# A bias table from a split bias, reciprocals spread by split diagonals, and the conformer's variance beside the last values' products

## The chip, the cores and the metric

The kernel runs on one core of a Trainium2 chip. The metric is device time in microseconds (us), the median of several executions. Within a core TensorE (PE) multiplies matrices, VectorE (DVE), ScalarE (ACT) and GpSimd (POOL) work on elements, and SyncE (SP) issues most of the loads. Each engine takes its instructions in the order of the program and waits for the others through semaphores.

## The reference

One layer of a hybrid decoder on 256 rows of width 2048, in float32:

```python
h = rms_norm(x, mix_norm_g[l])
q, kv, gate_logits, conv_in = jnp.split(h @ w_in[l], splits, axis=-1)
attn = nsa_attention(q, kv, gates, rel_bias, cmp_pos[l], cmp_w1[l], cmp_w2[l])
conv = conformer_conv(conv_in, conv_w[l], conv_b[l], conv_ln_g[l], conv_ln_b[l])
x = x + jnp.concatenate([attn, conv], axis=-1) @ w_out[l]
h = rms_norm(x, ffn_norm_g[l])
x = x + conv_glu_ffn(h, w_up[l], ffn_conv_w[l], ffn_conv_b[l], w_down[l])
```

and a last `rms_norm`. Attention has three branches (compressed, selected, window) and adds a bias to every score that depends on the distance of the two rows and the head, taken from a table of 32 buckets by 16 heads. The conformer part is a gated input, a causal convolution of 31 taps, a layer norm over 1024 channels and a swish:

```python
mu = jnp.mean(xf, axis=-1, keepdims=True)
xc = xf - mu
var = jnp.mean(xc * xc, axis=-1, keepdims=True)
y = xc * lax.rsqrt(var + NORM_EPS) * g.astype(jnp.float32) + b.astype(jnp.float32)
```

## The kernel before

The kernel works feature by feature: a tile has 128 features in the partitions and the 256 rows in the columns. Nearly all products are made in three float32r parts: both operands are split into a high part, rounded to float32r, and a low part, the float32 value less the high one, and the products high-high, high-low and low-high are summed in one PSUM bank. The weights stream in as chunks of 128 x 2048, are split on ACT (L126) and DVE or POOL (L131), and are used by PE one chunk after the other. A few small products use plain float32 operands, in one call each.

The stages follow each other on PE: the input projections (`tile_chunk`, L454 and L456), the compressed keys and values (L676 to L707), the values and gates, the queries with the attention mixed in, the output projection in sixteen chunks (`OUT_ORDER`; `mm_rows`, L189 to L191), the feed-forward up products (L1188, L1190) and the down products (L1207).

The order of the instructions on each engine is written out by the program. Small pieces of work stand in lists, and `hook` and `step`, called at fixed places among the large products, take one piece from each list at a time. Attention goes in ticks (`attn_tick`); a tick issues, for different units of a pipeline, the reciprocals, the scaling, the value products (`st_out`), the transposes, the scores and the exponentials. Output chunk 2 (the third of the sixteen) is the last chunk with ticks, and its fourth hook issues the last values' products.

The change touches four small pieces:

The bias table. `tab_neg` sets row 32 of the table to a large number and negates the others; `tab_rel` multiplies the 33 x 16 table with a 33 x 384 one-hot matrix (L388) in bank 4, copies the result and stores it to DRAM, from where `tab_load` reads it back spread over the partitions.

The conformer's variance. The squares of the centred channels are summed to one tile of 128 x 256 (`conf_fold`, L597); `conf_var` (L581) sums over the partitions by two products with that tile's halves as weights and a column of ones, so that the result lies with the rows in the partitions. `conf_norm` puts it third in the list `conf`, at the start of output chunk 2.

The conformer's spread. `conf_rstd` makes the reciprocal root (POOL, L603), `conf_diag` multiplies it into the identity matrix (L609), and `conf_spread` (L585) multiplies a matrix of ones with both diagonals: each of the 128 partitions then holds the 256 reciprocals. `conf_keep` copies them to SBUF, and `conf_apply` multiplies.

The second norm's spread. After the output projection `x2_rstd` does the same with the rows' mean squares (L221, L1092), and `x2_spread` (L1097), placed in the middle of the second chunk of the up products, multiplies with ones for each half. Between them DVE makes the low parts of the last four normalised tiles (`x2_evac`, L226).

Of the kernel before, what the change touches and what calls it, by code (L numbers as in the profile page):

```python
# [11 lines left out]
F32 = mybir.dt.float32  # L12
F32R = mybir.dt.float32r
AF = mybir.ActivationFunctionType
OP = mybir.AluOpType
PSUM = bass.MemoryType.PSUM

P = 128
T = 256
# [31 lines left out]
def hybrid_trunk(ctx: ExitStack, tc: tile.TileContext, a: dict, out: bass.AP):  # L51
    nc = tc.nc
    consts = ctx.enter_context(tc.tile_pool(name="consts", bufs=1))
    wpool = ctx.enter_context(tc.tile_pool(name="w", bufs=3))
    psum = ctx.enter_context(tc.tile_pool(name="ps", bufs=1, space=PSUM))
    bank = [psum.tile([P, 512], F32, name=f"bank{i}") for i in range(8)]
# [144 lines left out]

    ident = consts.tile([P, P], F32, name="ident")
    make_identity(nc, ident)
    ones = consts.tile([P, P], F32, name="ones")
    nc.vector.memset(ones, 1.0)
    half = consts.tile([P, 1], F32, name="half")
    nc.vector.memset(half, -0.5)
# [2 lines left out]
    def mean_of(pool, parts_, count, acc=EPS):  # L210

        for p_ in parts_:
            ms = pool.tile([P, 1], F32, name="ms", bufs=4)
            nc.vector.tensor_scalar(ms, p_, 1.0 / count, acc, op0=OP.mult, op1=OP.add)
            acc = ms
        return acc

    def rstd_of(pool, parts_, count, acc=EPS):

        r = pool.tile([P, 1], F32, name="rstd", bufs=2)  # L220
        nc.gpsimd.tensor_tensor(r, mean_of(pool, parts_, count, acc), half, op=OP.pow)  # L221
        return r

    def norm_evac(src, k, g):
        nc.scalar.activation(xt_h[:, k], src, AF.Copy, scale=g[:, k:k + 1])
        nc.vector.scalar_tensor_tensor(xt_l[:, k], src, g[:, k:k + 1], xt_h[:, k].bitcast(F32),  # L226
                                       op0=OP.mult, op1=OP.subtract)
# [3 lines left out]
    mixp = ctx.enter_context(tc.tile_pool(name="mix", bufs=1))  # L231
# [5 lines left out]
    with ExitStack() as mx:  # L237
        ap = mx.enter_context(tc.tile_pool(name="ap", bufs=1))
        wk = mx.enter_context(tc.tile_pool(name="wk", bufs=2))


        oh = ap.tile([33, 512], F32, name="oh", tag="oh")
        rbn = ap.tile([33, 16], F32, name="rbn")
        cw = ap.tile([P, 8, TAPS + 3], F32, name="cw")
        w1 = ap.tile([P, 16, 2, HD], F32, name="w1", tag="w1")
        w2 = ap.tile([P, HD], F32, name="w2")
# [132 lines left out]
        alive = ap.tile([P, 1], F32, name="alive")  # L379
        wb = mixp.tile([P, 16, T], F32, name="wb", tag="x2")  # L380

        def tab_neg():
            nc.vector.memset(rbn[32:33], BIG)
            nc.scalar.activation(rbn[:32], rbn[:32], AF.Copy, scale=-1.0)

        def tab_rel():
            pr = bank[4]
            nc.tensor.matmul(pr[:16, :384], rbn, oh[:, P:], start=True, stop=True)  # L388
            rtab = wk.tile([16, 384], F32, name="rtab", tag="e", bufs=6)
            nc.vector.tensor_copy(rtab, pr[:16, :384])  # L390
            nc.scalar.dma_start(scratch, rtab)
# [71 lines left out]
        summed, cf = [], {}  # L463
# [60 lines left out]
        for j in range(8):  # L524
# [34 lines left out]
            else:  # L559
                sg = []  # L560
# [8 lines left out]
        def conf_keep(scale=1.0):  # L569
            cf["k"] = wk.tile([P, T], F32, name="ck", tag="sg")  # L570
            nc.scalar.activation(cf["k"], cf["b"], AF.Copy, scale=scale)
# [6 lines left out]
        def conf_var():  # L578
            cf["b"] = bank[6][:, :T]
            for t in range(2):  # L580
                nc.tensor.matmul(cf["b"][:, t:t + 1], cf["s"][:, 0, t * P:(t + 1) * P], ones[:, :1],  # L581
                                 start=True, stop=True)

        def conf_spread():
            nc.tensor.matmul(cf["b"], ones, cf["d"].rearrange("p t c -> p (t c)"), start=True, stop=True)  # L585
            conf_keep()

        def conf_apply(op, j0, n=2):
            nc.vector.tensor_tensor(y[:, j0:j0 + n], y[:, j0:j0 + n], cf["k"][:, None].to_broadcast([P, n, T]), op=op)
# [14 lines left out]
            cf["r"] = rv  # L604

        def conf_diag():
            cf["d"] = wk.tile([P, 2, P], F32, name="dg", tag="sg")
            for t in range(2):
                nc.vector.tensor_scalar_mul(cf["d"][:, t], ident, cf["r"][:, t:t + 1])  # L609

        def conf_swish(j0):
            for j in range(j0, j0 + 4):
# [10 lines left out]
        no = lambda: None  # L623
# [8 lines left out]

        def conf_norm():
            conf.extend((
                no, no, conf_var, no, conf_rstd, no, conf_diag, no, conf_spread, no,
                *[lambda j=j: conf_apply(OP.mult, j) for j in (0, 2, 4, 6)],
                lambda: conf_swish(0), lambda: conf_swish(4), lambda: conf_split(0), lambda: conf_split(4)))

# [232 lines left out]
        def cmp_tr(m):  # L871
            for t in range(2):
                nc.tensor.matmul(bank[TR_BANKS[t]][:, 384:], pcb[:, t].rearrange("p s n -> p (s n)"), ident,
                                 is_transpose=True, start=True, stop=True)

        def cmp_store(m):
            if m == 0:
                cm["t"] = ap.tile([P, 4, T], F32, name="pct", tag="oh")
            for t in range(2):
                nc.scalar.activation(cm["t"][:, m, t * P:(t + 1) * P], bank[TR_BANKS[t]][:, 384:], AF.Copy)  # L880
            cbst["done"] = m + 1
# [5 lines left out]


        TR_BANKS = (3, 6)
        units = [(i, r, br) for i in range(8) for r in range(2) for br in range(2)]  # L890
        US = {}

# [50 lines left out]
        def st_transpose(n):  # L943
            e = US[n][0]
            pt = bank[TR_BANKS[n % 2]]
            for b in range(3):
# [3 lines left out]
        def st_evac(n):  # L950
            es = wk.tile([P, 384], F32, name="es", bufs=6)
            nc.scalar.activation(es, bank[TR_BANKS[n % 2]][:, :384], AF.Copy)
            US[n] = es

        def st_out(n):
            i = n // 4
            if n % 4 < 3:
                return
            o, q, m = bank[7], i // 4, i // 2
            assert cbst["done"] > m  # L960
            kw = dict(skip_group_check=True)
            for br in range(2):
                es = [US.pop(4 * i + 2 * r + br) for r in range(2)]
                for b, cols in enumerate((slice(0, T), slice(P, T))):
                    for r in range(2):
                        nc.tensor.matmul(o[64 * r:64 * r + 64, cols], vt[:, b, br, q, r],  # L966
                                         es[r][:, :T] if b == 0 else es[r][:, T:], start=br + b == 0, stop=False, **kw)
            for r in range(2):
                nc.tensor.matmul(o[64 * r:64 * r + 64, :T], vc[:, i % 2, q, r], cm["t"][:, m], start=False, stop=True,
                                 **kw)  # L970
            nc.scalar.activation(ma_h[:, i], o[:, :T], AF.Copy)
            nc.vector.tensor_sub(ma_l[:, i], o[:, :T], ma_h[:, i].bitcast(F32))
# [88 lines left out]
        def x2_evac(k):  # L1061
            norm_evac(x2_at(k), k, ffn_g)

        for n, (qr, g) in enumerate(OUT_ORDER):
            if n == 1:
                assert tick["n"] > NU - 2
            if n == 2:
                x2 = mixp.tile([P, 2, D], F32, name="x2")
                nc.scalar.dma_start(ffn_g, a["vecs"][:, :KD])
                for t in range(2):  # L1070
                    nc.scalar.dma_start(x2[:, t], x_rows[:, t])
            if n == 2:
                conf_norm()
            if n == 3:
                assert tick["n"] == NU + DEEP
                st["lag"] = False
            if n == 8:
                step(count=99)
            ws = w_next(2)
            for t in range(2):  # L1080
                out_part(n, ws, qr, g, t)
                if g == 3:
                    steps.append(lambda qr=qr, t=t: out_resid(qr, t))
            if g == 3 and qr < 3:
                steps.extend([lambda: None] * 2 + [lambda qr=qr: (x2_tr(qr, 0), x2_tr(qr, 1))]
                             + [lambda k=k: (x2_evac(k), x2_evac(k + 1)) for k in range(4 * qr, 4 * qr + 4, 2)])
        acc = [mean_of(mixp, [ss2[:, t, i:i + 1] for i in range(3)], D) for t in range(2)]
        step(count=99)
        dg = mixp.tile([P, 2, P], F32, name="dg2")
        def x2_rstd(t):  # L1090
            r2 = rstd_of(mixp, [ss2[:, t, 3:4]], D, acc[t])
            nc.vector.tensor_scalar_mul(dg[:, t], ident, r2)  # L1092

        def x2_spread():

            for t in range(2):
                nc.tensor.matmul(bank[4][:, t * P:(t + 1) * P], ones, dg[:, t], start=True, stop=True)  # L1097
            nc.scalar.activation(rB, bank[4][:, :T], AF.Copy)


    with ExitStack() as fx:
        fp = fx.enter_context(tc.tile_pool(name="fp", bufs=1))
# [6 lines left out]
                                          ap=[[0, P], [1, D]]))  # L1109
# [57 lines left out]
                    stages.remove(q)  # L1167


        for t in range(2):  # L1170
            x2_rstd(t)
        between = {(0, 6): lambda: (x2_tr(3, 0), x2_tr(3, 1)),
# [3 lines left out]
        for m in range(NFT // 2):  # L1176
# [3 lines left out]
            for part in range(2):  # L1180
                bk = UP_BANKS[2 * ((2 * m + part) % 4):][:2]
                for kh in range(2):
                    wh, wl = [w.rearrange("p (k c) -> p k c", c=256) for w in w_next(1 if m + part + kh else 2)]
                    up_stages()
                    for n, (k, i) in enumerate((k, i) for k in range(8) for i in range(2)):
# [3 lines left out]
                                         start=kt == 0, stop=False)  # L1189
# [190 lines left out]
```

## Time and profile before

| what | us |
|---|---|
| median of 3 runs (1095.45 to 1095.52) | 1095.48 |
| the profiled execution | 1095.29 |
| its span, from first to last instruction | 1093.5 |
| PE busy | 1084.9 |
| DVE busy | 791.0 |
| ACT busy | 602.2 |
| POOL busy | 186.8 |

PE's records overlap, since matmuls are pipelined, so busy time alone doesn't say what a product costs. The chain of waits follows the work that ended last back to the start; the length of a piece on it is the time that the piece holds up the end. The line of a piece is that of the source; "x4" means four records of the profile.

### The profile page before, as it was taken

The numbers are of one execution on the slowest core, as the hardware profiler recorded it, in microseconds if no ns is written. First come the engines' busy times: TensorE is split into PE (matmuls) and PEld (weight loads), VectorE is DVE, ScalarE is ACT, GpSimd is POOL, SyncE is SP. The second block draws the span as 40 slices with busy tenths as digits, with TensorE's granted clock in tenths as the row PEclk, the third lists the DMA queues.
The fourth block names the chain that finished last, engine by engine and source line by source line (L and its number), as shares of the span: only waits on it lengthen the run. The fifth ranks groups of instructions, "written<-read, shape, count | busy, mean of one in ns | idle before, by whom it ended". The sixth has DMA issues, their size and how long they took to land.

```text
span 1093.5 us, 16270 instructions
## 1 busy us (share of the span) xinstructions
PE 1084.9 (99%) x6418; PEld 947.6 (87%) x6418; DVE 791.0 (72%) x1318; ACT 602.2 (55%) x915; POOL 186.8 (17%) x139
## 2 busy tenths in 40 slices
PE   9999999999999999999999999999999999999997
PEld 9888899887788888888888888888888888888886
DVE  7799989875656677777777777777777655665675
ACT  7644667887645555555555555545555544544552
POOL 0898775766000000000000000000000000000000
PEclk9999999999999999999999999999999999999999
DMA  9677535323654655555555555555554555556642
GB/s 363 241 265 261 178 127 174 116 78 138 248 193 166 237 186 192 191 190 192 193 192 193 193 188 186 187 186 186 189 191 151 193 188 189 198 179 203 232 161 77
DMA packets 34216, 207.55 MB, mean 190 GB/s; under 512 B 3883, under 2 KB 6715, under 8 KB 14428
## 3 DMA queue, kind: packets, MB, share of 16 engines
q1 hardware_dynamic: 30620, 199.46, 51.8%
q10 hardware_dynamic: 3520, 7.06, 1.8%
q8 instruction: 50, 0.82, 0.3%
q14 instruction: 26, 0.21, 0.1%
HBM read 204.39 MB, written 2.12 MB: 189 GB/s over the span
## 4 chain that ended last, share of the span: by engine, by line
PE 96%; DVE 2%; ACT 1%; issue 1%; POOLq 0%; POOL 0%; DVEq 0%; ACTq 0%
PE bank L1188 30%; PE bank L1207 17%; PE bank L1190 15%; PE bank L454 9%; PE bank L456 5%; PE bank L189 3%; PE bank L191 3%; PE bank L190 3%; PE bank L198 1%; PE bank L196 1%; PE bank L966 1%; PE bank L197 1%; PE bank L199 1%; PE bank L947 1%; PE bank L167 1%
## 5 line engine op out<-in xcount | busy, mean ns | idle before, releaser
L126 ACT ACTIVATE wh<-wraw 128x1024 fp32r<-128x1024 f32 (+3 forms) x248 | 355.8, 1452 | 344.5 <-issue 136.6
L131 DVE TENSOR_TENSOR wl<-wraw,wh 128x2048 fp32r<-128x2048 f32 (+2 forms) x194 | 361.7, 1873 | 206.1 <-ACT wh L126 206.1
L1188 PE MATMUL bank<-xt,wh 128*128 128x512 f32 x1408 | 488.5, 394 | 0.0
L1190 PE MATMUL bank<-xt,wl 128*128 128x256 f32 x1408 | 390.1, 277 | 0.0
L1188 PEld LDWEIGHTS bank<-xt,wh 128*128 128x128 f32 x1408 | 264.0, 188 | 61.2
L1190 PEld LDWEIGHTS bank<-xt,wl 128*128 128x128 f32 x1408 | 264.4, 188 | 0.0
L454 PE MATMUL bank<-xt,wh 128*128 128x512 f32 x464 | 150.6, 395 | 0.0
L1244 POOL TENSOR_TENSOR rstd<-ss,half 128x1 f32<-128x1 f32 x2 | 1.1, 548 | 730.4 <-DVE ss L1241 730.4
L131 POOL TENSOR_TENSOR wl<-wraw,wh 128x1024 fp32r<-128x1024 f32 (+1 forms) x54 | 121.2, 2271 | 19.8 <-ACT wh L126 15.3
L456 PE MATMUL bank<-xt,wl 128*128 128x256 f32 x464 | 105.8, 280 | 0.0
L489 DVE SCALAR_TENSOR_TENSOR bank<-us,cw,bank 128x256 f32<-128x256 f32 x232 | 95.0, 481 | 4.2 <-ACT bank L484 3.5
L454 PEld LDWEIGHTS bank<-xt,wh 128*128 128x128 f32 x464 | 80.8, 188 | 12.8 <-issue 0.6
L456 PEld LDWEIGHTS bank<-xt,wl 128*128 128x128 f32 x464 | 83.5, 188 | 8.4
L1207 PE MATMUL bank<-wl,gh 128*128 128x512 f32 x352 | 89.9, 336 | 0.0
L1207 PE MATMUL bank<-wh,gl 128*128 128x512 f32 x352 | 89.8, 336 | 0.0
L1207 PE MATMUL bank<-wh,gh 128*128 128x512 f32 x352 | 89.8, 336 | 0.0
L1151 DVE SCALAR_TENSOR_TENSOR yt<-u,fcw,yt 128x255 f32<-128x255 f32 (+1 forms) x176 | 80.9, 480 | 3.1
L941 POOL TENSOR_SCALAR e<-e,lsum 128x128 f32<-128x128 f32 x64 | 59.2, 940 | 36.3 <-ACT qs L824 15.7
L1207 PEld LDWEIGHTS bank<-wl,gh 128*128 128x128 f32 x352 | 54.1, 188 | 7.0
L1207 PEld LDWEIGHTS bank<-wh,gl 128*128 128x128 f32 x352 | 54.1, 188 | 6.9
L1207 PEld LDWEIGHTS bank<-wh,gh 128*128 128x128 f32 x352 | 54.0, 188 | 6.9
L1147 ACT ACTIVATE yt<-u,fcw 128x256 f32<-128x256 f32 x88 | 47.4, 586 | 0.0
(222 smaller groups left out, 1237.8 us busy)
## 6 DMA issues: line engine op xcount, KB each, us to landing
wraw<-in_w_u SPq DMA_DIRECT2D x88, 1024.0 KB, 4.8
wraw<-in_w_d SPq DMA_DIRECT2D x44, 768.0 KB, 4.2
wraw<-in_w_t SPq DMA_DIRECT2D x29, 1024.0 KB, 5.0
wraw<-in_w_o SPq DMA_DIRECT2D x16, 1024.0 KB, 5.0
wraw<-in_w_dl SPq DMA_DIRECT2D x11, 1024.0 KB, 4.8
wraw<-in_w_vg SPq DMA_DIRECT2D x4, 608.0 KB, 4.5
hb<-in_head SPq DMA_DIRECT2D x2, 1024.0 KB, 10.9
xr<-in_x SPq DMA_DIRECT2D x2, 1024.0 KB, 19.0
```

The lines of the kernel that those rows point to most:

```text
L126: nc.scalar.activation(h[:, sl], raw[:, sl], AF.Copy)
L131: (nc.gpsimd if pooled else nc.vector).tensor_sub(l[:, sl], raw[:, sl], h[:, sl].bitcast(F32))
L189: nc.tensor.matmul(ps, xh, wh, start=first, stop=False)
L454: nc.tensor.matmul(ps, wh[:, sl], xt[:, kt].rearrange("p a t -> p (a t)"), start=kt == 0, stop=False)
L456: nc.tensor.matmul(ps[:, T:], wl[:, sl], xt_h[:, kt], start=False, stop=kt == KD - 1)
L489: nc.vector.scalar_tensor_tensor(y[:, j] if last else acc[0], us[:, j, k:k + T], cw[:, j, k:k + 1], acc[0], op0=OP.mult, op1=OP.add)
L941: nc.gpsimd.tensor_scalar_mul(e[:, lo:hi], e[:, lo:hi], lsum[:, br, t:t + 1])
L1147: nc.scalar.activation(yt, us_[i], AF.Identity, scale=fcw[:, c, 2:3], bias=fcw[:, c, 3:4])
L1151: nc.vector.scalar_tensor_tensor(ys[i][:, d:], us_[i][:, :T - d], fcw[:, c, k:k + 1], ys[i][:, d:], op0=OP.mult, op1=OP.add)
L1188: nc.tensor.matmul(bk[i], wh[:, k, sl], xt[:, kt].rearrange("p a t -> p (a t)"), start=kt == 0, stop=False)
L1190: nc.tensor.matmul(bk[i][:, T:], wl[:, k, sl], xt_h[:, kt], start=False, stop=kt == KD - 1)
L1207: nc.tensor.matmul(banks[n][:, :hi - lo], g[p][:, kt % 4, sl], ws[w][:, k * DW + lo:k * DW + hi], start=kt + i == 0, stop=i == 2 and kt == ...
```

## The change

`ones` becomes a float32r tile of which float32 users take a view. `tab_neg` splits the table in a rounded part and the rest and rounds the one-hot matrix; `tab_rel` makes two float32r products. `diag_split` makes a rounded diagonal and its rest; both spreads make two float32r products with ones over 256 columns. `conf_var` is made in four products with half as many columns of the sums as weights, and instead of its place in the list it is issued at the head of the last values' products. The diagonals of the second norm move from the pool of the whole kernel to that of the feed-forward stage.

```diff
-    ones = consts.tile([P, P], F32, name="ones")
+    ones_r = consts.tile([P, P], F32R, name="ones")
+    ones = ones_r.bitcast(F32)
...
+    def diag_split(d, t, r):
+        nc.vector.tensor_scalar_mul(d[0][:, t], ident, r)
+        nc.vector.scalar_tensor_tensor(d[1][:, t], ident, r, d[0][:, t].bitcast(F32), op0=OP.mult, op1=OP.subtract)
...
+        rbs = ap.tile([33, 2, 16], F32R, name="rbs")
...
         def tab_neg():
             nc.vector.memset(rbn[32:33], BIG)
             nc.scalar.activation(rbn[:32], rbn[:32], AF.Copy, scale=-1.0)
+            nc.scalar.activation(rbs[:, 0], rbn, AF.Copy)
+            ohr.append(wk.tile([33, 384], F32R, name="ohr", tag="e", bufs=6))
+            nc.scalar.activation(ohr[0], oh[:, P:], AF.Copy)
+            nc.vector.tensor_sub(rbs[:, 1], rbn, rbs[:, 0].bitcast(F32))
 
         def tab_rel():
             pr = bank[4]
-            nc.tensor.matmul(pr[:16, :384], rbn, oh[:, P:], start=True, stop=True)
+            for n in range(2):
+                nc.tensor.matmul(pr[:16, :384], rbs[:, n], ohr[0], start=n == 0, stop=n == 1)
...
         def conf_var():
             cf["b"] = bank[6][:, :T]
             for t in range(2):
-                nc.tensor.matmul(cf["b"][:, t:t + 1], cf["s"][:, 0, t * P:(t + 1) * P], ones[:, :1],
-                                 start=True, stop=True)
+                for h in range(0, P, 64):
+                    nc.tensor.matmul(cf["b"][h:h + 64, t:t + 1], cf["s"][:, 0, t * P + h:t * P + h + 64], ones[:, :1],
+                                     start=True, stop=True)
 
         def conf_spread():
-            nc.tensor.matmul(cf["b"], ones, cf["d"].rearrange("p t c -> p (t c)"), start=True, stop=True)
+            for n, d in enumerate(cf["d"]):
+                nc.tensor.matmul(cf["b"], ones_r, d.rearrange("p t c -> p (t c)"), start=n == 0, stop=n == 1)
             conf_keep()
...
         def conf_diag():
-            cf["d"] = wk.tile([P, 2, P], F32, name="dg", tag="sg")
+            cf["d"] = [wk.tile([P, 2, P], F32R, name=nm, tag="sg") for nm in ("dg_h", "dg_l")]
             for t in range(2):
-                nc.vector.tensor_scalar_mul(cf["d"][:, t], ident, cf["r"][:, t:t + 1])
+                diag_split(cf["d"], t, cf["r"][:, t:t + 1])
...
-                no, no, conf_var, no, conf_rstd, no, conf_diag, no, conf_spread, no,
+                no, no, no, no, conf_rstd, no, conf_diag, no, conf_spread, no,
...
+        beside = []
...
+            while beside:
+                beside.pop(0)()
             o, q, m = bank[7], i // 4, i // 2
...
+            if n == 2:
+                beside.append(conf_var)
...
-        dg = mixp.tile([P, 2, P], F32, name="dg2")
         def x2_rstd(t):
             r2 = rstd_of(mixp, [ss2[:, t, 3:4]], D, acc[t])
-            nc.vector.tensor_scalar_mul(dg[:, t], ident, r2)
+            diag_split(dg, t, r2)
 
         def x2_spread():
 
-            for t in range(2):
-                nc.tensor.matmul(bank[4][:, t * P:(t + 1) * P], ones, dg[:, t], start=True, stop=True)
+            for n, d in enumerate(dg):
+                nc.tensor.matmul(bank[4][:, :T], ones_r, d.rearrange("p t c -> p (t c)"), start=n == 0, stop=n == 1)
...
+        dg = [fp.tile([P, 2, P], F32R, name=nm) for nm in ("dg2_h", "dg2_l")]
```

More of the change, by code (lines that the diff above doesn't have):

```diff
@@ L380, in hybrid_trunk @@
         wb = mixp.tile([P, 16, T], F32, name="wb", tag="x2")
+        ohr = []
         def tab_neg():
```

## The prediction

> **What bounds the kernel now.** I read the page's head and its chain by engine first, to see which engine sets the end; then the chain in order of time around each edited product, because there a product's whole price stands, with what it delays behind it; then the timelines of the other engines around the edits, for the cover.
>
> ```profile
> span 1093.5 us, 16270 instructions
> PE 1084.9 (99%) x6418; PEld 947.6 (87%) x6418; DVE 791.0 (72%) x1318; ACT 602.2 (55%) x915; POOL 186.8 (17%) x139
> PE 96%; DVE 2%; ACT 1%; issue 1%; POOLq 0%; POOL 0%; DVEq 0%; ACTq 0%
> ```
>
> PE (TensorE) carries 96% of the chain that ends last, so a microsecond of PE work taken out at nearly any place is a microsecond off the end, and work added to DVE (VectorE) or ACT (ScalarE) costs nothing while it stays ahead of PE. The question is then how many PE microseconds the four edited products hold. The chain shows each beside its neighbours (columns: start, length on the chain, what).
>
> ```profile
> 68.43 0.74 PE bank L388 x2
> 69.17 0.43 PE bank L454
> ...
> 69.72 0.23 PE bank L454
> ...
> 272.03 0.23 PE bank L191
> 272.27 0.34 PE bank L581 x4
> 272.61 0.34 PE bank L189
> ...
> 283.19 0.43 PE bank L585 x2
> 283.62 0.23 PE bank L189
> ...
> 362.30 0.45 PE bank L1097 x4
> 362.75 0.23 PE bank L1188
> ```
>
> L388 is the bias table, L581 the conformer's variance, L585 the spread of its reciprocal, L1097 the spread of the second norm's reciprocal. A neighbour that takes 0.23 in the stream takes 0.43 behind the table and 0.34 behind the variance; that surplus belongs to the product ahead of it. So the four cost 0.74 + 0.20 = 0.94, 0.34 + 0.11 = 0.45, 0.43 and 0.45 us: 2.27 us in all. That is the ceiling of what the change can give back on PE, reached only if the new products were free.
>
> Two rates follow. One float32 call leaves two records, and L585's two records of 256 columns take 0.43, so 0.84 ns a column and record. L454 is float32r, one record for a call: 512 columns in 0.23, 0.45 ns a column.
>
> **Part one, the bias table.** One float32 product of 384 columns becomes two float32r products of 384. Streaming: before 2 x 384 x 0.84 ns = 0.645 us, after 2 x 384 x 0.45 ns = 0.35 us. The other 0.94 - 0.645 = 0.295 us is neither: it is what surrounds a product of this shape.
>
> ```profile
> L388 PE MATMUL bank<-oh,rbn x2: 483/488/492, 68.4 to 68.7; 33*16 33x384 f32 x2
> 69.10 0.19 PEld L454 LDWEIGHTS bank<-xt,wh 128*128 128x128 f32 x1 [0.64 <-issue]
> ```
>
> The product uses 33 rows and 16 columns of the array, and the next weights, elsewhere loaded ahead, are loaded only at 69.10, after 0.64 us in which nothing was loaded. The new products have the same 33 by 16 shape, but no float32r product in this trace has any shape but 128 by 128, so whether the surround stays is unknown. Bounds: if it stays, 0.35 + 0.295 = 0.645 and the saving is 0.295; if it goes, 0.35 and the saving is 0.59. A loss would need the surround to double on the second product: 0.35 + 0.59 = 0.94, saving zero. I take 0.30, because the row it is nearest to is its own, with the same shape.
>
> The Trainium skill, page TensorEngine Tiling (Array Packing), section Key Properties, says that a change of the tiling mode drains the engine. The late weight load above is such a drain, but the trace can't show whether a float32r product of this shape still is a change of mode; by the rule it is, and the sum is the one below, while without a drain it would be 0.29 us more.
>
> What feeds it is new: on ACT a copy of the 33 x 16 table and a copy of the 33 x 384 one-hot, on DVE a subtraction of 33 x 16.
>
> ```profile
> 61.86 0.20 ACT L384 ACTIVATE rbn<-rbn 32x16 f32<-32x16 f32 x1
> 63.60 0.39 ACT L181 ACTIVATE us<-bank 128x256 f32<-128x256 f32 x1 [1.54 <-PE bank L456]
> ...
> 267.01 0.88 ACT L952 ACTIVATE es<-bank 128x384 f32<-128x384 f32 x2
> ...
> 61.56 0.07 DVE L383 MEMSET rbn<- 1x16 f32 x1
> 69.04 0.88 DVE L489 SCALAR_TENSOR_TENSOR bank<-us,cw,bank 128x256 f32<-128x256 f32 x2 [0.66 <-ACT bank L484]
> ...
> 130.00:150.00 20.00, 20.00 (x176) 18.06 (x171) 15.13 (x39) 13.49 (x30) 11.75 (x7) 1.00 0.23 77
> ```
>
> ACT: 0.20 for the small copy, 0.44 for 384 columns (half of L952's 0.88): 0.64 us into the 1.54 us that it stands idle before 63.60. DVE: its subtraction stands right behind the memset of 61.56 and needs ACT's rounded copy, which ends at 61.86 + 0.20 + 0.20 = 62.26, or at 62.70 if it also waits for the one-hot copy. DVE then stands for 0.7 to 1.1 us, with the convolution taps (L489) queued behind it and ACT's next first tap (L484) waiting for those. DVE has 0.66 us idle at 69.04 and 4.87 us between 130 and 150, and in this stretch the weights' low parts are made on POOL (GpSimd), so PE waits for nothing in that queue. Cost nothing; without that cover 0.7 to 1.1 us.
>
> **Part two, the variance.** Two float32 products of 128-wide weights on one column become four of 64-wide weights: eight records instead of four. They are moved from the third step slot of the conformer's list in output chunk 2 to the head of the last values' group (L966), about 2 us later; no DMA is issued with them, and no wait moves: the last sum of squares began at 201.4, the bank's last transpose was copied out at 271.4, and the reader L601 runs at 280.20.
>
> ```profile
> L597 DVE TENSOR_TENSOR s<-s x4: 419/685/686, 180.1 to 201.4; 128x512 f32<-128x512 f32 x3, 128x256 f32<-128x256 f32 x1
> 270.53 0.91 ACT L952 ACTIVATE es<-bank 128x384 f32<-128x384 f32 x2 [2.64 <-PE bank L947]
> 129.03 2.23 PE bank L676 x64
> 147.29 0.38 PE bank L707 x16
> 205.41 0.92 PE bank L843 x8
> L966 PE MATMUL bank<-es,vt x128: 272/326/431, 200.5 to 275.3; 128*64 128x256 f32 x64, 128*64 128x128 f32 x64
> ```
>
> No row has 64-wide weights on one column. Nearest is L676 (64-wide weights alternating between the array's halves, 75 columns): 2.23/64 = 0.035 a record, so 0.28 for eight. Below it L707 (32-wide): 0.38/16 = 0.024, 0.19 for eight. Above it L843 (128-wide weights, 32 columns): 0.92/8 = 0.115, 0.92 for eight, if the halves do not load side by side. L966 already uses the 128 by 64 shape, so no further change of shape enters. I take 0.28: saving 0.45 - 0.28 = 0.17, bounds -0.47 to +0.26.
>
> The skill speaks against this edit: the same page, section Instruction Overhead, gives a matmul some 60 cycles whatever its columns, and advises against tiling for a dimension that is already small. At 0.84 ns a column that is an estimated 0.05 us a record and 0.40 for eight, a saving of 0.05 and a sum of 0.77 instead of 0.89; L676's 0.035 a record, with more columns than 60, disagrees.
>
> **Parts three and four, the two spreads.** Each becomes two float32r products of 256 columns: 2 x 0.116 = 0.23 us. The shape stays 128 by 128 and the neighbours there already show 0.23, so nothing else is left in them: 0.43 - 0.23 = 0.20 and 0.45 - 0.23 = 0.22. Bounds: zero if changing the type costs what it saves, otherwise these.
>
> Each diagonal now has a second part on DVE, one scalar_tensor_tensor of 128 x 128. The 128 x 128 row here takes 0.29 and the 128 x 256 one of that operation (L489) 0.48, so between these; I take 0.35.
>
> ```profile
> 179.49 0.69 DVE L589 TENSOR_TENSOR y<-y,ck 128x512 f32<-128x512 f32 x1
> ...
> 280.20 0.15 DVE L601 TENSOR_SCALAR rv<-bank 128x2 f32<-128x2 f32 x1
> 281.04 0.29 DVE L609 TENSOR_SCALAR dg<-ident,rv 128x128 f32<-128x128 f32 x1 [0.69 <-POOL rv L603]
> 281.56 0.29 DVE L609 TENSOR_SCALAR dg<-ident,rv 128x128 f32<-128x128 f32 x1 [0.23 <-POOL rv L603]
> 283.03 0.59 PE L585 MATMUL bank<-dg,ones 128*128 128x256 f32 x2
> ...
> 355.42 0.29 DVE L1092 TENSOR_SCALAR dg<-ident,rstd 128x128 f32<-128x128 f32 x1 [0.66 <-POOL rstd L221]
> 356.49 0.29 DVE L1092 TENSOR_SCALAR dg<-ident,rstd 128x128 f32<-128x128 f32 x1 [0.66 <-POOL rstd L221]
> 357.89 0.88 DVE L226 SCALAR_TENSOR_TENSOR xt<-bank,ffn_g,xt 128x256 fp32r<-128x256 f32 x2
> 361.79 0.40 PE L1188 MATMUL bank<-xt,wh 128*128 128x512 f32 x1
> 362.14 0.61 PE L1097 MATMUL bank<-dg,ones 128*128 128x128 f32 x4
> ```
>
> Conformer: diagonals done at 281.85 before; the first low part takes up the 0.23 idle and 0.12 more, the second adds 0.35: 282.3. PE asks at 283.03; 0.7 us are left. The pair takes both buffers of its ring; the second was the mean's, last read at 179.49. Second norm: 0.7 us more on DVE ahead of the last four normalised tiles (L226), which end at 359.5 instead of 358.8; the first PE use of them is at 361.79, so 2.3 us are left. The new diagonals lie in the feed-forward stage's memory, which the mixing stage held; its last user in the trace is the square on ACT (355.46), where DVE begins anyway. Cost nothing; without cover 0.5 and 0.7 us.
>
> **The sum.** 0.30 + 0.17 + 0.20 + 0.22 = 0.89 us. The profiled execution took 1095.29 us, its span 1093.5 and 1.79 around it; it becomes 1094.40. The median of the runs is 0.19 above that execution: 1095.48 - 0.89 = 1094.59, so **1094.6 us**. With the bounds of the table (0 to 0.59) and of the variance (-0.47 to 0.26), the spreads at 0.42, the likeliest case spans a loss of 0.05 to a gain of 1.27 us, 1094.2 to 1095.5.
>
> **The rivals.**
>
> *The table's part is swallowed in attention.* Between 186 and 260 the chain runs for long through DVE and ACT, and PE waits there twice visibly.
>
> ```profile
> 196.76 0.36 PE L905 MATMUL bank<-k_h,qs 128*128 128x256 f32 x1 [0.34 <-DVE mn L915]
> 236.91 0.29 DVE e L915
> 258.57 0.51 PE bank L189
> ```
>
> If those waits end at a time that PE's earlier products do not set, the 0.30 gained at 68 us is lost at 196.76 and 0.59 remain: 1094.9. Against it: at 236.91 the chain enters DVE from a PE product, so DVE starts earlier when PE does. Chance 0.2.
>
> *The surround goes and the small products cost less than taken:* 0.59 + 0.26 + 0.42 = 1.27 us, 1094.2. Against it, the unchanged 33 by 16 shape. Chance 0.12.
>
> *Slower: the second norm's low parts come late.* Were the feed-forward memory of the new diagonals held by a later user than the square, DVE would stand with the last four normalised tiles queued behind it, and PE would stop at 361.79. It decides from a wait of 2.3 us on; from 2.3 + 0.89 = 3.2 us on the kernel is slower than before, and at 5.4 us by 0.2%. With a wait of 4 us: 1095.48 - 0.89 + 1.7 = 1096.3. For it, the move of the tile; against it, that PE's last product on the mixing tiles ends before DVE begins. Chance 0.05.
>
> *It doesn't do what it says:* a change of type costs on PE what the passes save, or the eight small records cost 0.92. Then gains and losses meet near zero, about 1095.4. Chance 0.08.
>
> **How the numbers follow.** The forecast has 0.55. What a measurement of this kernel can tell from no change is about 0.2%, 2.2 us; the four products hold 2.27 us, and the new ones must stream 0.35 + 0.23 + 0.23 us at least, so faster by over 0.2% needs a gain outside the four: 0.03. Slower by over 0.2% is the tail of the slower rival with whatever else the shifted order brings: 0.03. Within: 0.94. The range runs from 1093.9, the best case less the 0.34 us wait at 196.76 should the shift close it, to 1095.6, just beyond the likeliest case's worst; that leaves out most of the slower rival and a little on each side.
>
> **What would show it.** Right: on the chain the table at 0.65 with its surround, the variance's eight records within 0.3 at the head of the last values' group, and 0.23 for each spread, the instructions around them unchanged; DVE idle ahead of a 33 x 16 subtraction near 62 us. Wrong: weights loaded ahead behind the table (no drain); eight records of 0.1 us; PE idle at the spreads or ahead of the twelfth input tile; a longer wait at 196 or 258 us than now.

## The result, and the profile after

The changed kernel took 1111.02 us (median of 5 runs, 1103.67 to 1113.01) against 1095.45 us before (1095.29 to 1095.52): a ratio of 1.0127, 95% interval 1.0113 to 1.0142. It is slower by 15.6 us where 0.9 us less was predicted, and it scatters over 9 us where the kernel before repeats within 0.25. The profiled execution is the shortest of the five.

The head of its page and the two groups of the up products, high and low parts, answer to the page before (groups: count, busy us, mean ns of one):

```profile
span 1101.9 us, 16283 instructions
PE 1092.8 (99%) x6420; PEld 950.8 (86%) x6420; DVE 792.6 (72%) x1323; ACT 603.1 (55%) x917; POOL 186.7 (17%) x139
PE 97%; DVE 1%; ACT 1%; issue 1%; DMA 0%; POOLq 0%; POOL 0%; ACTq 0%
L1208 PE MATMUL bank<-xt,wh 128*128 128x512 f32 x1408 | 497.7, 399 | 0.0
L1210 PE MATMUL bank<-xt,wl 128*128 128x256 f32 x1408 | 395.4, 281 | 0.0
```

PE is still the bound, and its added time is not in the edited products but in the up products behind them. Before, the same groups were busy for less:

```profile
L1188 PE MATMUL bank<-xt,wh 128*128 128x512 f32 x1408 | 488.5, 394 | 0.0
L1190 PE MATMUL bank<-xt,wl 128*128 128x256 f32 x1408 | 390.1, 277 | 0.0
```

The table of stretches, for 400 to 800 us, first of the kernel before and then of the changed one (the stretch and its length; busy us and count of PE, its weight loads, DVE, ACT and POOL; PE's granted clock, 1.00 being the full one; the DMA's share and GB/s):

```profile
400.00:800.00 400.00, 400.00 (x2310) 349.79 (x2309) 295.22 (x397) 204.49 (x255) 0.00 (x0) 1.00 0.54 190
```

```profile
400.00:800.00 400.00, 400.00 (x2266) 346.91 (x2265) 290.72 (x391) 199.60 (x249) 0.00 (x0) 1.00 0.52 185
```

PE never idles and its clock is granted in full in both, yet it does 2266 products in the time of 2310. From start to start a pair (512 and 256 columns) takes 346.7 ns before and 353.3 ns after, the same in every stretch of 20 us from 380 to 820 us. The changed kernel has the longer interval from the transposes on, seven pairs into the up products; over the 1400 pairs from there the 6.6 ns are 9.2 us.

The chain of waits of the changed kernel at the four edits, which the prediction priced:

```profile
68.62 0.44 PE bank L401 x2
69.07 0.43 PE bank L467
...
273.50 0.33 PE bank L595 x8
273.82 1.36 PE bank L984 x16
...
282.81 0.24 PE bank L600 x2
...
361.45 0.23 PE bank L1116 x2
361.69 0.23 PE bank L1208
```

These came out as worked out. The table is 0.44 + 0.20 = 0.64 us (0.645 predicted), the two spreads 0.24 and 0.23 (0.23 each), the variance 0.33 with 0.09 less in the values' group behind it, so 0.24 (0.28 predicted). PE starts the up products at 351.62 instead of 352.55. So in this execution 0.9 us is gained up to there and 9.1 lost in the up products: 1093.5 - 0.9 + 9.1 = 1101.7 of its 1101.9.

That leaves the scatter, up to 7 us or more above this execution. What it is made of showed only in the second trace of the same kernel (e4, below).

### The profile page after: what moved, and what is told of

The parts are those of the page before. It is cut to its first block, busy times and chain, and to the rows that moved or that the text cites. A ratio compares the mean times of both kernels' runs of the same rounds, so it can differ in the third digit from the quotient of the medians.

```text
span 1101.9 us, 16283 instructions
## 1 busy us (share of the span) xinstructions
PE 1092.8 (99%) x6420; PEld 950.8 (86%) x6420; DVE 792.6 (72%) x1323; ACT 603.1 (55%) x917; POOL 186.7 (17%) x139
## 4 chain that ended last, share of the span: by engine, by line
PE 97%; DVE 1%; ACT 1%; issue 1%; DMA 0%; POOLq 0%; POOL 0%; ACTq 0%
PE bank L1208 30%; PE bank L1227 17%; PE bank L1210 15%; PE bank L467 9%; PE bank L469 5%; PE bank L189 3%; PE bank L191 3%; PE bank L190 3%; PE bank L198 1%; PE bank L196 1%; PE bank L984 1%; PE bank L963 1%; PE bank L199 1%; PE bank L197 1%; PE bank L167 1%
## 5 line engine op out<-in xcount | busy, mean ns | idle before, releaser
L1208 PE MATMUL bank<-xt,wh 128*128 128x512 f32 x1408 | 497.7, 399 | 0.0
L1210 PE MATMUL bank<-xt,wl 128*128 128x256 f32 x1408 | 395.4, 281 | 0.0
L467 PE MATMUL bank<-xt,wh 128*128 128x512 f32 x464 | 150.7, 396 | 0.0
L469 PE MATMUL bank<-xt,wl 128*128 128x256 f32 x464 | 105.8, 280 | 0.0
L469 PEld LDWEIGHTS bank<-xt,wl 128*128 128x128 f32 x464 | 83.5, 188 | 8.4
```

The lines of the kernel that those rows point to most:

```text
L467: nc.tensor.matmul(ps, wh[:, sl], xt[:, kt].rearrange("p a t -> p (a t)"), start=kt == 0, stop=False)
L469: nc.tensor.matmul(ps[:, T:], wl[:, sl], xt_h[:, kt], start=False, stop=kt == KD - 1)
L1208: nc.tensor.matmul(bk[i], wh[:, k, sl], xt[:, kt].rearrange("p a t -> p (a t)"), start=kt == 0, stop=False)
L1210: nc.tensor.matmul(bk[i][:, T:], wl[:, k, sl], xt_h[:, kt], start=False, stop=kt == KD - 1)
```

## The experiments

All ran beside the kernel before, at 1095.41, 1095.28 and 1095.40 us in the three groups.

### First group: is it the second norm's spread, its place in memory, or the earlier edits?

**e1**: the second norm's spread whole again.

```diff
-            diag_split(dg, t, r2)
+            nc.vector.tensor_scalar_mul(dg[:, t], ident, r2)
...
-            for n, d in enumerate(dg):
-                nc.tensor.matmul(bank[4][:, :T], ones_r, d.rearrange("p t c -> p (t c)"), start=n == 0, stop=n == 1)
+            for t in range(2):
+                nc.tensor.matmul(bank[4][:, t * P:(t + 1) * P], ones, dg[:, t], start=True, stop=True)
...
-        dg = [fp.tile([P, 2, P], F32R, name=nm) for nm in ("dg2_h", "dg2_l")]
+        dg = fp.tile([P, 2, P], F32, name="dg2")
```

> The changed kernel with the second norm's spread made whole again: one float32 diagonal, two float32 products of 128 columns; the diagonal's tile stays in the feed-forward stage's memory, the three other edits stay. Rate theory (the up products run at one of a few steady rates, which is settled anew at each break, a product of float32 operands or a transpose among the float32r ones, and then holds; the split spread is no break): the float32 spread is a break again, all pairs behind it take 346.7 ns as before or another constant rate; with 346.7 the time is 1094.5 us and repeats within 0.2 us. Place theory (the moved diagonals shift tiles in memory and PE's reads collide): 353 ns a pair and 1103 us or more, since the tile stays moved. Shift theory (the three earlier edits alone bring PE to the up products at another moment): 353 ns or more at least up to the spread.

Measured: 1096.96 us (1094.61 to 1101.81, 12 runs). The twelve times fall into four heaps: four at 1094.6 to 1094.7, three at 1096.9 to 1097.0, one at 1098.6, four at 1101.7 to 1101.8. The pairs are at 346.7 ns behind the spread, as the rate theory had it, and at 353.3 between the transposes and the spread, as the shift theory had it for that stretch. So the earlier edits change the rate too, but only up to the spread, which sets it anew. The rate is back; a scatter in steps is left, which no theory named.

**e2**: the kernel before with only the second norm's spread split (the same edit turned round).

> The kernel before with only the second norm's spread changed: split diagonals in the feed-forward stage's memory, two float32r products of 256 columns. Rate theory: the transposes ahead of the spread left the pairs at 346.7 ns in the kernel before, and nothing up to there is changed, so the pairs stay at 346.7 and the time is 1095.45 - 0.22 = 1095.2 us. Place theory: 353 ns a pair from the transposes on, 1103 us or more. Shift theory: as the rate theory, 1095.2 us.

Measured: 1104.31 us (1104.27 to 1104.62), ratio 1.0082 [1.0069, 1.0095]. The pairs run at 346.7 ns between the transposes and the spread, and at 353.3 from the spread on. All the theories' numbers for this run miss in one part: the split spread itself changes the rate, which "no break" had excluded, and moved memory cannot be it, since the pairs ahead of the spread are fast. There is no scatter here.

**e3**: one float32 product of one column behind the split spread.

```diff
+            nc.tensor.matmul(bank[5][:, :1], ones, ones[:, :1], start=True, stop=True)
             nc.scalar.activation(rB, bank[4][:, :T], AF.Copy)
```

> The changed kernel with one more product behind the split spread: float32, ones by one column of ones, into a free bank; its result is read by nobody. Rate theory: this is a break, the pairs behind it settle anew, at 346.7 ns (1094.8 us, 0.2 to 0.3 for the product and its two records) or at another constant rate; the pairs between the transposes and the spread stay at 353. Place and shift theories: nothing changes, 353 ns a pair and 1104 to 1113 us.

Measured: 1110.98 us (1107.69 to 1111.07); the pairs stay at 353.3 ns. A float32 product as such does not bring the rate back.

**e4**: the changed kernel again.

> The changed kernel once more, unchanged but for an empty line at its end, for a second trace of it. Rate theory: each execution keeps one rate over all up pairs behind the transposes, and its time is 1094.5 us plus 1408 times the rate's excess over 346.7 ns; a time of 1111 us belongs to about 358 ns. Place and shift theories: the excess changes from chunk to chunk within an execution, with the buffers in use.

Measured: 1109.12 us (1107.55 to 1110.75); in its trace the pairs are at 353.3 ns exactly as in the first trace, so the expected 358 is wrong, and the further 7 us arise ahead of the up products: they begin at 358.65 instead of 351.62. DVE's timeline near the table, first in the first trace of the changed kernel, then in e4 (start, us, engine, line, operation; in brackets the idle time before it):

```profile
61.72 1.33 DVE L396 TENSOR_TENSOR rbs<-rbn,rbs 33x16 fp32r<-33x16 f32 x1 [0.71 <-ACT rbs L393]
51.19 18.93 POOL L131 TENSOR_TENSOR wl<-wraw,wh 128x1024 fp32r<-128x1024 f32 x8
```

```profile
61.70 8.39 DVE L396 TENSOR_TENSOR rbs<-rbn,rbs 33x16 fp32r<-33x16 f32 x1 [0.71 <-ACT rbs L393]
51.12 18.96 POOL L131 TENSOR_TENSOR wl<-wraw,wh 128x1024 fp32r<-128x1024 f32 x8
```

A subtraction of 33 x 16 elements takes 1.33 us in one execution and 8.39 in the other. POOL's eight splits take 18.96 / 8 = 2.37 us each; from 51.12 the fifth ends at 62.97 and the eighth at 70.08. The subtraction ends at 63.05 in the one trace and at 70.09 in the other, in e1 at 65.3 (3.71 us): each time at the end of a split. It waits out the split that runs and none, one or three more. PE's timeline of e4 shows where DVE's lateness comes out:

```profile
70.15 0.35 PE L401 MATMUL bank<-ohr,rbs 33*16 33x384 f32 x1 [1.39 <-DVE rbs L396]
...
133.44 0.74 PE L691 MATMUL bank<-tok,w 128*64 128x75 f32 x16 [1.06 <-ACT tok L670]
...
180.79 0.70 PE L588 MATMUL bank<-ysum,ones 128*128 128x256 f32 x2 [2.15 <-DVE alive L817]
```

The table's second product waits for the subtraction; later the compressed keys wait for values that DVE evacuates, and the conformer's mean for the taps queued on DVE. The three waits come to 4.6 of the 7 us. Most of the rest is lost behind the first of them, where PE does not wait but its granted clock falls. In e4 its mean over 70 to 72 us is 0.74 of the full one, in the first trace 1.00. The stretch from 72 to 80 us, in the first trace and in e4:

```profile
72.00:80.00 8.00, 8.00 (x47) 7.01 (x46) 7.83 (x21) 5.36 (x8) 6.35 (x3) 1.00 0.76 269
```

```profile
72.00:80.00 8.00, 8.00 (x41) 6.92 (x40) 7.27 (x20) 1.67 (x4) 0.00 (x0) 0.85 0.28 115
```

The table's second product starts at 68.74 in the one trace and at 70.15 in the other, 1.4 us later; the same low product (L469) that starts at 77.34 in the one starts at 80.40 in the other, 3.1 us later.

The Trainium skill, page SBUF — State Buffer, section SBUF: two separate sides, tells of a port pair that DVE and GpSimd share as an exclusive lock for a whole instruction: between a DVE operation with two inputs in SBUF and a GpSimd operation that reads SBUF, the one that starts first has it and the other blocks until it is done. The waits above agree. In one point the traces are narrower: behind POOL's scaling (one tensor in, and it reads SBUF too) DVE is hardly held up. In the kernel before, a split of DVE with both inputs in SBUF starts at 258.43, 0.69 us ahead of the end of two scalings, and takes 1.31 us where 1.22 is usual:

```profile
257.62 1.50 POOL L941 TENSOR_SCALAR e<-e,lsum 128x128 f32<-128x128 f32 x2
258.43 1.31 DVE L131 TENSOR_TENSOR wl<-wraw,wh 128x1024 fp32r<-128x1024 f32 x1
```

The other way round POOL waits, which agrees: where DVE's splits are under way, four scalings take 5.89 us, twice what two pairs of 1.50 come to:

```profile
264.47 5.89 POOL L941 TENSOR_SCALAR e<-e,lsum 128x128 f32<-128x128 f32 x4 [1.27 <-DVE lsum L935]
264.20 1.22 DVE L131 TENSOR_TENSOR wl<-wraw,wh 128x1024 fp32r<-128x1024 f32 x1
267.30 2.35 DVE L131 TENSOR_TENSOR wl<-wraw,wh 128x1024 fp32r<-128x1024 f32 x2
```

### Second group: the lock by itself, and the rate by itself

**e5**: e1, and the subtraction reads its rounded operand from PSUM.

```diff
-            nc.vector.tensor_sub(rbs[:, 1], rbn, rbs[:, 0].bitcast(F32))
+            nc.scalar.activation(bank[4][:33, 496:512], rbs[:, 0].bitcast(F32), AF.Copy)
+            nc.vector.tensor_sub(rbs[:, 1], rbn, bank[4][:33, 496:512])
```

> The changed kernel with two edits: the second norm's spread whole in float32 again (as in e1), and the table's subtraction on DVE reads its rounded operand from a PSUM bank, where ACT puts a second copy, so that only one of its operands lies in SBUF. Lock theory (a DVE instruction with both operands in SBUF waits while POOL splits weights there, for one or more whole POOL instructions of 2.4 us, and the lateness of DVE reaches PE at the table's second product, the compressed keys and the conformer's mean): the subtraction takes under 0.4 us, PE stalls nowhere over 0.7 us, the pairs run at 346.7 ns, 1094.7 us repeating within 0.2. Rival (the subtraction is slow for another reason, a 33-row float32r result for one): it still takes 1.3 to 8.4 us and the time still scatters from 1094.6 to 1101.8.

Measured: 1094.98 us (1094.87 to 1095.41, 11 runs), ratio 0.9998 [0.9989, 1.0006]; no PE wait above 0.3 us but the one for the first loads, at 1.04 us, which the kernel before has too. The line of the subtraction:

```profile
L397 DVE TENSOR_TENSOR rbs<-rbn,bank x1: 164/164/164, 62.2 to 62.2; 33x16 fp32r<-33x16 f32 x1
```

It takes 0.16 us. Against e1 only the place of one operand differs, and ACT's copy that puts it there; the twelve times of e1 spread over 7.2 us, the eleven of e5 over 0.5 (0.2 was expected).

**e6**: only the detour through PSUM.

> The changed kernel with only the table's subtraction changed as in e5; the split spread stays. Lock theory and rate theory together: the early scatter is gone and the pairs stay at 353.3 ns, so 1095.45 - 0.95 + 1400 x 6.6 ns = 1103.7 us, repeating within 0.3. If the early scatter and the up products' rate had one cause, both would go: 1094.5.

Measured: 1103.95 us (1103.88 to 1103.98), ratio 1.0079 [1.0065, 1.0093]; the pairs at 353.3 ns and the subtraction at 0.17 us. Two causes, then, that add up: 8.7 us more than the kernel before here and 6.8 in e7, against 15.6 in the changed kernel.

**e7**: the kernel before with only the table's edit.

> The kernel before with only the table's edit (split table, rounded one-hot, two float32r products). Lock theory: the scatter belongs to this edit alone, 1095.45 - 0.30 = 1095.15 us where the subtraction gets through after one POOL instruction, and up to 7.1 us more where it waits for four: 1095.2, 1097.5, 1099 or 1102.3. Rival (it needs the other edits): 1095.15, repeating within 0.2.

Measured: 1102.12 us (1102.03 to 1102.42), ratio 1.0063 [1.0049, 1.0077]; the subtraction takes 8.37 us, up to the end of POOL's row of splits. This edit alone brings the loss; that it would scatter did not come true, all five times lie where the longest wait puts them. The pairs are at 346.7 ns.

**e8**: e6 with the split spread as four products of 128 columns.

```diff
-            for n, d in enumerate(dg):
-                nc.tensor.matmul(bank[4][:, :T], ones_r, d.rearrange("p t c -> p (t c)"), start=n == 0, stop=n == 1)
+            for t in range(2):
+                for n, d in enumerate(dg):
+                    nc.tensor.matmul(bank[4][:, t * P:(t + 1) * P], ones_r, d[:, t], start=n == 0, stop=n == 1)
```

> The kernel of e6 with the split spread as four float32r products of 128 columns instead of two of 256: the same columns and operands, another sequence. Rate theory in its general form (the rate is settled by the sequence ahead of the pairs, whatever its type): the rate may change, to 346.7 ns and 1094.5 us, or stay. If only float32 products bring the pairs back to 346.7: 353.3 ns, 1103.7 us.

Measured: 1104.27 us (1104.13 to 1104.36), ratio 1.0082 [1.0068, 1.0096]; 353.3 ns. By itself this would fit "only float32 brings it back".

### Third group: what sets the rate

**e9**: e6 with the split spread one pair later.

```diff
-                   (0, 8): lambda: (x2_evac(14), x2_evac(15), w_pump()), (1, 8): x2_spread}
+                   (0, 8): lambda: (x2_evac(14), x2_evac(15), w_pump()), (1, 9): x2_spread}
```

> The kernel of e6 with the split spread one pair of up products later. If the rate hangs on the moment within the pairs' own cycle at which the two 256-column products come: another of the rates is possible, 346.7 ns and 1094.6 us among them. If the sequence of widths alone settles it (the same one, one pair later): 353.3 ns and 1104.0 us.

Measured: 1094.79 us (1094.71 to 1094.89, 10 runs), ratio 0.9994 [0.9985, 1.0004]. One pair's shift takes 9.2 us off. The line of the high products and the stretch that was compared above:

```profile
L1209 PE MATMUL bank<-xt,wh x1408: 391/391/487, 351.6 to 840.6; 128*128 128x512 f32 x176
400.00:800.00 400.00, 400.00 (x2310) 352.69 (x2309) 295.73 (x397) 204.05 (x252) 0.00 (x0) 1.00 0.53 190
```

**e10**: e6 with two float32 products of 128 columns behind the spread, read by nobody.

```diff
+            for t in range(2):
+                nc.tensor.matmul(bank[5][:, t * P:(t + 1) * P], ones, ident, start=True, stop=True)
             nc.scalar.activation(rB, bank[4][:, :T], AF.Copy)
```

> The kernel of e6 with two more products behind the split spread, float32, 128 columns each, ones by the identity, into a free bank that nobody reads: the form of the whole spread as work for nothing. Rate theory (the last break ahead of the pairs settles the rate, and this form leaves 346.7 ns, as in the kernel before, e1, e5 and e7): 346.7 ns, 1103.95 - 9.1 + 0.43 = 1095.3 us. If the rate hung on the split operands, or on what stands where in memory: 353.3 ns and 1104.4 us.

Measured: 1095.17 us (1095.05 to 1095.28), ratio 0.9998 [0.9988, 1.0007]; 346.7 ns. Work for nothing takes 8.8 us off, so neither the split operands nor their place is to blame.

**e11**: e6 with the two products one pair apart.

```diff
-                   ..., (1, 8): x2_spread}
+                   ..., (1, 8): lambda: x2_spread(0), (1, 9): lambda: x2_spread(1)}
```

`x2_spread(n)` here makes the n-th of the two products, and the copy of the result with the second.

> The kernel of e6 with the two products of the split spread apart, the first where both stand now, the second one pair later: a sequence of widths that no run has shown. Rate theory: one of the rates, held to the end of the up products: 346.7 ns and 1094.6 us, faster than the kernel before and than e5, or 353.3 ns and 1104.0 us. It has no reason for either.

Measured: 1094.82 us (1094.62 to 1094.92), ratio 0.9994 [0.9985, 1.0003]; 346.7 ns.

Read to the nanosecond from the traces, start to start, the pairs repeat fixed cycles: 350, 349, 361 ns in the changed kernel (mean 353.3), 350 and 343 or 344 in the kernel before and in e11, 347, 347, 346 in e9 and e10 (all 346.7).

**e12**: e7 with five weight chunks taken from POOL.

```diff
-        pooled = POOLED[0] <= c < POOLED[1]
+        pooled = POOLED[0] <= c < POOLED[1] and not 9 <= c < 14
```

> The kernel of e7 (only the table's edit) with five of POOL's weight chunks, those split around the table's subtraction, given to DVE. For the duration of one instruction, not for the time, since DVE has some 10 us more work. Lock theory: POOL is idle when the subtraction comes, and it takes under 0.4 us. Rival (a slow form of instruction): 1.3 us or more.

Measured: one run, 1107.8 us, with more work on DVE as said. The instruction in question, and ahead of it the first two of the splits that went to DVE:

```profile
L391 DVE TENSOR_TENSOR rbs<-rbn,rbs x1: 168/168/168, 65.4 to 65.4; 33x16 fp32r<-33x16 f32 x1
50.06 3.30 DVE L131 TENSOR_TENSOR wl<-wraw,wh 128x1024 fp32r<-128x1024 f32 x2
```

0.17 us, POOL idle: the form of the instruction is not slow, POOL's splits are what it waited for. The two splits on DVE show the same wait: the first starts while POOL's last one ahead of its pause runs, which ends at 51.15, and they take 3.30 us where two take 2.35 elsewhere.

## Why the prediction was wrong

**What held.** The ceiling and each term on PE: the table's surround stayed (0.30 of gain), the eight small records cost 0.03 to 0.04 each and not 0.1 (they stand at the head of the values' group, which has the same 128 by 64 shape and got 0.09 us shorter), and the spreads fell to 0.23 and 0.24. With the two other effects removed, e9 has all four parts of the change. PE begins the up products 1.0 us earlier than before and ends 1.1 earlier; some 0.9 was forecast. The median gains 0.6 us: the interval of the ratio includes 1, but each of e9's ten times lies below each of the 25 beside it. The rest of the gain is lost behind the last ACT instruction, from where the trace of e9 has 4.45 us to its end and that of the kernel before 3.87. The covers for the diagonals held too: PE waited at neither spread.

**First step that failed: "DVE then stands for 0.7 to 1.1 us ... PE waits for nothing in that queue. Cost nothing; without that cover 0.7 to 1.1 us."** The wait for ACT came as priced (0.71 us). Not priced was the subtraction itself, taken for a small instruction by its size. It is the only DVE instruction of that stretch with both operands in SBUF while POOL splits weights, and the same splits were named in that step as cover for PE; the taps and evacuations around it read one operand from PSUM. It stood 1.33 to 8.39 us (e4), 0.16 with one operand in PSUM (e5), 0.17 with POOL idle (e12). The cover named in that step, 0.66 us at 69 and 4.87 us after 130, is enough for 1.3 us and not for 8.4: up to 7 us reach PE, at the table's second product, the compressed keys and the conformer's mean, and by the lower clock behind such a wait. The kernel before has a row of such a meeting, which the step did not use: a multiplication of `gates` by `alive`, 128 x 16 and both in SBUF, beside POOL's splits. In e12 the same instruction (L811 there) comes when POOL is idle. Two rows of the kernel before, then the one of e12:

```profile
165.14 9.48 POOL L131 TENSOR_TENSOR wl<-wraw,wh 128x1024 fp32r<-128x1024 f32 x4 [0.73 <-ACT wh L126]
172.99 1.97 DVE L803 TENSOR_SCALAR gates<-gates,alive 128x16 f32<-128x16 f32 x1
```

```profile
184.85 0.24 DVE L811 TENSOR_SCALAR gates<-gates,alive 128x16 f32<-128x16 f32 x1
```

1.97 against 0.24 us: POOL's last split ends at 174.62 and the multiplication at 174.96. That row puts a price of some 1.7 us of waiting on such an instruction beside one split; that it can be four splits, no row of the kernel before shows.

**Second step that failed: the spreads' "nothing else is left in them", with the bound "zero if changing the type costs what it saves".** It priced a product by itself and its neighbours, and took the pairs behind it as fixed at their rate. They are not: the same 1408 pairs run at 346.7 or 353.3 ns, for 489 or 498 us, and which of the two depends on what interrupts them last and at which pair. The kernel before shows both rates, the slower one for the seven pairs from 352.55 to the transposes at 355.02 and the faster one behind them; the prediction did not read these intervals. In the changed kernel it is the other way round: the first seven pairs are fast, and the slow rate begins at the transposes and stays behind the spread. The split spread where the change puts it leaves the slow rate, whether the pairs ahead of it are slow (the changed kernel twice, e6) or fast (e2); whole in float32 it leaves the fast one, from fast pairs (before) or slow ones (e1, e5, e7); one pair later, split, the fast one (e9).

**The rivals.** None of them named either mechanism. The slower one looked for DVE's lateness at the second norm, where there was none; the time lost to DVE was lost 290 us earlier. A loss of over 0.2% was given 0.03, as that rival's tail "with whatever else the shifted order brings"; the 2.27 us that the four products hold bound the gain and say nothing of a loss, and no row was read for its size.

**What stays open.** Why a given sequence ends in one cycle or the other: neither the type (e3 and e10 are both float32, with opposite ends), nor the widths alone (e9 has those of e6) decides it, and no rule was found that tells the end ahead of a run. Why the subtraction gets through after one split in some executions and after four in others is open too. So is the 1113.01 us run of the changed kernel, whose trace was not kept: its mean granted clock is the lowest of the five, 0.995 against 0.996 to 0.998, so the clock may have a part in it, which is not shown. Why the clock falls behind one wait and not behind another (in e1 it stays at 1.00 behind a wait of 2.0 us) and why e9 loses 0.6 us behind the last ACT instruction were not tested.

## What to carry to other kernels

Before a small instruction is put on DVE beside a busy POOL, see where its operands lie: with two in SBUF against a POOL instruction that has two as well, its price here was POOL's instructions and not its own, and one operand in PSUM avoided it. Look through the kernel as it is for an instruction that already pays that price, one whose time is far above that of its size. And where a long run of equal products sets the end, look at the interval from start to start and not at the busy share: at 99% busy the rate can differ by 2%, and moving an interruption by one pair can be worth more than the interruption itself.

## What the runs showed of the hardware that was not expected

A stream of alternating 512- and 256-column float32r products has at least two steady rates, 346.7 and 353.3 ns a pair, each a fixed cycle of pairs, kept over 80 and more weight chunks and the same in both traces of the changed kernel. DVE with two SBUF operands waits for a two-operand POOL instruction to end (1.33, 3.71, 8.37 to 8.39 us seen) and hardly for a one-operand one (1.31 us for a split that starts during a scaling), while such a scaling waits for DVE (four in 5.89 us, twice the usual). Behind a PE wait of 1.39 us the granted clock was 0.74 of the full one in the mean of 70 to 72 us and 0.85 in that of 72 to 80 (e4), behind one of 2.0 us it stayed at 1.00 (e1). The variance's four 64-wide products, eight records, fit into 0.33 us at the head of a group of the same shape.
